# Seven products instead of plain matmuls for half of the second layer's last six channel tiles, and the mixer's coefficients computed earlier

## The chip, the cores and the metric

The kernel runs on one core of one Trainium2 chip. The metric is the device time of one execution in microseconds; the kernel before took 2144.43 us in the median of three runs (2143.85 to 2144.75). A profiled execution lies beside them and gives the views that are quoted here.

The core has five engines with queues of their own: TensorE (PE, with its weight loads as PEld), VectorE (DVE), ScalarE (ACT), GpSimd (POOL) and SyncE (SP). SP's queue issues nearly all DMAs, one after the other.

## What is computed

Two layers on 1024 tokens of 1024 channels, all in fp32. Each layer is a mixer (the first retention beside a gated delta rule, the second a gated linear recurrence) and a convolutional feed-forward block, both with residuals and RMS norms, and there is a norm at the end. Cut to what matters here:

```python
def rglru_mixer(hn, w_in, conv_w, conv_b, w_a, b_a, w_x, b_x, lam, w_out):
    ...
    r = jax.nn.sigmoid(jnp.einsum('btni,nij->btnj', xb, w_a) ... + b_a)
    i = jax.nn.sigmoid(jnp.einsum('btni,nij->btnj', xb, w_x) ... + b_x)
    log_a = -LRU_C * r * jax.nn.softplus(-lam)
    ...

def conv_ffn(hn, w_up, conv_w, conv_b, w_down):
    up = causal_dwconv(hn @ w_up, conv_w) + conv_b
    gate, val = jnp.split(up, 2, axis=-1)
    return (jax.nn.silu(gate) * val) @ w_down      # 2816 hidden channels to 1024

def reference(...):
    for layer in range(2):
        h = h + mixer(rms_norm(h, norm_mix[layer]))
        h = h + conv_ffn(rms_norm(h, norm_ffn[layer]), ...)
    return rms_norm(h, norm_final)
```

`softplus(-lam)`, `b_a` and `b_x` give the mixer's coefficients, a few columns of eight values.

## The kernel before, in words

Activations lie transposed, channels on the 128 partitions and tokens along the free axis: the residual is eight tiles `H[0]` to `H[7]` of 128x1024. Every fp32 matmul is made of three in the fast format: each operand is split into a high and a low part (ScalarE casts the high part, VectorE subtracts to get the low one), and `mm3` (L316 to L321) adds high x high, high x low and low x high into one PSUM bank.

**Seven products.** Where it can, the kernel takes a block of 2 x 2 matrices by seven products instead of eight (Strassen's scheme with few additions). The rows of the block are two groups of k tiles of the hidden channels, the columns are the even and the odd 256-token quarters (j = 0 and 1), and the outputs are a pair of output tiles. Seven operands, numbered o = 0 to 6, are made of the four blocks of activations and used for all pairs; `load_pair` (L283 on) makes the seven weight operands of a pair on VectorE. `pair_product` issues one product: three matmuls of 512 columns for each of its k tiles. `pair_added` adds each product into `H` on VectorE (L820).

**Feed-forward.** `ffn` first runs the up projection in 22 pairs p of output tiles (gate and value), 84 matmuls each; pair 0 in halves, since the norm's row comes late. After each pair, `hidden` computes the convolution and the gate and `store_parts` writes what the down projection will need to DRAM: ready splits to `p_dram` (high and low, L880), raw combinations to `s_dram` (L881), plain values to `y_dram`. The 22 hidden tiles make three sets c for the down projection: tiles 0 to 7, 8 to 15, and 16 to 21. `load_set(c, o)` brings operand o of a set back into SBUF, either as a ready split (L914) or raw, with a cast and a subtraction to follow (L922, L924, L925). The loads of set 0 begin while the last up pairs run, those of the next set while the fourth pair of outputs of the set before runs (`following` and `plain` say after which product).

In the first layer the third set is done by seven products too. In the second layer its six tiles are split whole by `store_parts` (L594, L595), written to `l_dram` (L870), loaded by `load_parts` (L931), and used by `final`: for each of the eight output tiles 6 k tiles, plain, in three column parts of 512, 256 and 256 tokens, with the residual added (L553) and squared (L407) as each tile is done. The norm of a part is `norm_beside` for the first (VectorE transposes and sums, a round through DRAM, the power on GpSimd: no TensorE), `norm_tok` and `norm_row` for the other two: strips of ones sum over partitions on TensorE (L480), VectorE turns them (L470, L471), GpSimd takes the power (L472), TensorE spreads the result as a row (L489). The tiles of a finished part are scaled (L1046) and stored between the tiles of the part that follows; of the first part every second one goes to ScalarE and GpSimd.

**Coefficients.** `lru_small` computes the second mixer's columns, some 29 operations of 128x8 on VectorE with one activation on ScalarE. It is called in the first layer's down projection, set 1, behind its first pair, into one of the four buffers of the pool `kept`.

**Order.** A scheduler places the instructions on each engine's queue by the order in which they were written and by when buffers come free, so a load can stand well ahead of the place that calls it; engines then work strictly through their queues. SP's queue holds all loads and stores of the places named here. The weights come six quarters ahead, in seven raw buffers.

Of the kernel before, what the change touches and what calls it, by code (L numbers as in the profile page):

```python
# [103 lines left out]
class Block:  # L104
    def __init__(self, ctx, tc, I, out, stop=None):
        self.ctx, self.tc, self.nc, self.I, self.out = ctx, tc, tc.nc, I, out
        nc = tc.nc
        pool = lambda n, b, **k: ctx.enter_context(tc.tile_pool(name=n, bufs=b, **k))
        self.perm = pool("perm", 1)
        self.wraw_p = pool("wraw", 7)  # L110
        self.kept = pool("kept", 4)
        self.parts = pool("parts", 1)
        self.wsp = pool("wsp", RING)
        self.tp = pool("tp", 3)
        self.sm = pool("sm", 2)
# [71 lines left out]
    def quarter_order(self):  # L187
# [10 lines left out]
        for layer in range(2):  # L198
# [11 lines left out]
            if layer == 0:  # L210
                o += [(("ffn_v0", t), 7) for t in range(4)]
# [611 lines left out]
    def ffn(self, layer, gain):  # L823
        nc, I = self.nc, self.I
        V, A = nc.vector, nc.scalar
        third = gain is not None
        sets = 3 if third else 2
        y_dram = self.tc.dram_tile([NPAIR, P, T], F32, name=f"yf_dram{layer}")
        s_dram = self.tc.dram_tile([sets, 5, 4, P, HALF], F32, name=f"sf_dram{layer}")

        p_dram = self.tc.dram_tile([sets, 4, 4, 2, P, HALF], F32, name=f"pf_dram{layer}")
        if not third:
            l_dram = self.tc.dram_tile([NPAIR - 16, 2, P, T], F32, name=f"lf_dram{layer}")
        depth = lambda c: 4 if c < 2 else 3

        def where(c, o):

            if c == 0 or not third:
# [24 lines left out]
        def store_parts(p, y, hi):  # L863
# [44 lines left out]
        def load_set(c, o):  # L908
# [17 lines left out]

        def load_parts(p):
            places = self.place2(p - 16)
            for n in range(2):
                for e in range(2):  # L930
                    nc.sync.dma_start(f32(places[n][e]), l_dram[p - 16, e][:, n * HALF:(n + 1) * HALF])  # L931
            return places
# [6 lines left out]
        def hidden(p, tg):  # L939
            tv = conv(NPAIR + p, self.halo[1])  # L940
            V.tensor_tensor(tg, tg, tv, ALU.mult)  # L941
            if (third or p < 16) and p % 8 < depth(p // 8):
# [25 lines left out]
        ys = {}  # L968
        following = {0: {1: (4, 5), **{o: ((o + 4) % 7,) for o in range(2, 7)}},
                     1: {2: (0,), 3: (1, 2), 4: (3,), 5: (4,), 6: (5, 6)}}  # L970
        plain = {0: {1: (0, 1), **{o: (o,) for o in range(2, 7)}}, 1: {}}
        for c in range(sets):
            done = self.down_steps(gain) if c == 2 else {}
            for t in range(4):
                sums, banks = self.pair_added(t), {}
                key = (f"ffn_w{layer}", c, t) if c < 2 else (f"ffn_v{layer}", t)
                for o in range(7):
                    sums(o, self.pair_product(banks, o, self.quarter(key, o), x=where(c, o)))
                    if t == 3 and c < 2:
                        for q in (following if third else plain)[c].get(o, ()):  # L980
                            load_set(c + 1, q)
                    if not third and (c, t) == (1, 3) and o in (1, 2):
                        for p in range(16, 20) if o == 1 else (20, 21):
                            ys[p] = load_parts(p)
# [4 lines left out]
                if third and (c, t) == (1, 0):  # L989
                    self.lru_small()  # L990

        if not third:
            self.final([ys[p] for p in range(16, NPAIR)], f"ffn_d{layer}")
# [44 lines left out]
    def final(self, ys, name):  # L1038

        nc = self.nc  # L1040
        V = nc.vector

# [9 lines left out]
        def part(t0, w, left):  # L1052

            sl = slice(t0, t0 + w)
            st = {"whole": t0 == 0}

            def each(m, h):
# [3 lines left out]
            self.part(ys, name, self.groups(1), sl, each, kept)  # L1061
            return st, sl


        kept = {}
# [6 lines left out]
        late[2].append(lambda: run(self.norm_tok(s1[0], 256)))  # L1072
        late[4].append(lambda: run(self.norm_row(s1[0], w=256)))
        pr = lambda st: st["row"][:, 0:256]
        for k in range(5, KT):
            late[k] += [lambda j=j: scale(*s1, j, pr(s1[0])) for j in range(3 * (k - 5), min(3 * (k - 4), KT))]
        s2 = part(768, 256, late)
# [12 lines left out]
    def lru_small(self):  # L1090

        V = self.nc.vector
        room = self.kept.tile([P, HALF], F32, tag="kept", name="lcols")
# [6 lines left out]
        V.tensor_scalar(nl, self.cols_of("lru_lam"), -1.0, None, ALU.mult)  # L1100
# [3 lines left out]
        V.tensor_scalar(ba, self.cols_of("lru_ba"), 0.5, None, ALU.mult)  # L1104
        V.tensor_scalar(bx, self.cols_of("lru_bx"), 0.5, None, ALU.mult)
# [737 lines left out]
    def _mix0_out(self, gain, gd):  # L1843
# [56 lines left out]
def _inputs(a):  # L1900
# [26 lines left out]
    for l in range(2):  # L1927
# [3 lines left out]
        if l == 0:  # L1931
            n = w.shape[0] // P - 16
            ins["ffn_v0"] = np.ascontiguousarray(w[2 * D:].reshape(n, P, KT, P).transpose(2, 1, 0, 3)).reshape(KT, P, n * P)
        else:
# [27 lines left out]
```

## Time and profile before

| what | us |
|---|---|
| median of three runs | 2144.43 |
| profiled execution, its own time | 2143.45 |
| span of its trace | 2141.7 |
| TensorE busy | 2126.3 |
| VectorE busy | 1722.0 |
| ScalarE busy | 1079.5 |
| GpSimd busy | 100.2 |

The span goes from the first to the last instruction. Matmuls are pipelined: one of 512 columns lasts 0.39 us in the records while the next begins after some 0.23, so TensorE's busy time is no measure of its pace; starts are. The granted clock of TensorE is full in all slices of the page. A wait row names the engine that waited and what released it.

### The profile page before, as it was taken

How to read it: one execution, taken by the hardware profiler on the slowest of the kernel's cores; microseconds unless marked ns; L12 is line 12 of the kernel's file. 1: busy time of each engine (PE TensorE's matmuls, PEld its weight loads, DVE VectorE, ACT ScalarE, POOL GpSimd, SP SyncE). 2: the span in 40 equal slices, each digit the busy share in tenths (PEclk: the TensorE clock that was granted, in tenths of full speed). 3: DMA queues.
4: the chain of work that ended last, by engine and by line, in shares of the span. 5: the costliest groups of instructions: out<-in, count | busy, mean ns of one | idle time of the engine just before them, and what ended most of it. 6: DMA issues, size and time to landing. Idle time of an engine off the chain costs nothing.

```text
span 2141.7 us, 29752 instructions
## 1 busy us (share of the span) xinstructions
PE 2126.3 (99%) x10648; PEld 1771.1 (83%) x10648; DVE 1722.0 (80%) x2630; ACT 1079.5 (50%) x1752; POOL 100.2 (5%) x115
## 2 busy tenths in 40 slices
PE   9999999999999999999999999999999999999998
PEld 7878888888888888887888888888888888888887
DVE  7995677766999989988868786768998989888645
ACT  6444422235665555555324576756655555554222
POOL 0102122300000000000000000000000000000002
PEclk9999999999999999999999999999999999999999
DMA  5354444543145445548745212152354444375542
GB/s 188 91 170 126 137 94 94 170 141 117 50 169 180 156 137 185 172 168 293 234 160 172 72 59 78 64 159 63 123 187 163 150 152 175 118 269 180 178 170 85
DMA packets 242021, 313.23 MB, mean 146 GB/s; under 512 B 62432, under 2 KB 129424, under 8 KB 241872
## 3 DMA queue, kind: packets, MB, share of 16 engines
q1 hardware_dynamic: 205632, 304.15, 43.0%
q10 hardware_dynamic: 35088, 6.36, 1.5%
q8 instruction: 84, 1.38, 0.3%
q0 software_dynamic: 1152, 0.81, 0.2%
q14 instruction: 65, 0.53, 0.1%
HBM read 215.79 MB, written 95.45 MB: 145 GB/s over the span
## 4 chain that ended last, share of the span: by engine, by line
PE 65%; issue 30%; DMA 2%; DVE 2%; POOL 1%; SPq 0%; ACT 0%; POOLq 0%; DVEq 0%
PE ps L319 19%; PE ps L321 19%; PE ps L320 19%; PE pc L319 1%; PE pc L321 1%; PE pc L320 1%; DMA raw<-in_mix_in_dram 0%; DMA s<-pf_dram 0%; PE ps L1644 0%; DMA l<-gc_dram 0%; PE pc L1552 0%; PE ps L1596 0%; PE pc L1664 0%; PE ps L1694 0%; PE pc L1578 0%
## 5 line engine op out<-in xcount | busy, mean ns | idle before, releaser
L319 PE MATMUL ps<-s,whi 128*128 128x512 f32 (+1 forms) x2692 | 1048.4, 390 | 1.0 <-ACT s L924 0.6
L320 PE MATMUL ps<-s,whi 128*128 128x512 f32 (+1 forms) x2692 | 1043.9, 388 | 1.9 <-DVE s L925 1.8
L321 PE MATMUL ps<-s,wlo 128*128 128x512 f32 (+1 forms) x2692 | 1042.6, 388 | 0.6 <-DVE wlo L273 0.6
L272 ACT CAST whi<-raw 128x512 fp32r<-128x512 f32 (+2 forms) x616 | 374.0, 613 | 607.7 <-PE ps L320 470.3
L319 PEld LDWEIGHTS ps<-s,whi 128*128 128x128 f32 x2692 | 505.6, 188 | 106.3 <-issue 1.8
L320 PEld LDWEIGHTS ps<-s,whi 128*128 128x128 f32 x2692 | 505.8, 188 | 105.6 <-DVE s L925 4.6
L321 PEld LDWEIGHTS ps<-s,wlo 128*128 128x128 f32 x2692 | 505.6, 188 | 104.4 <-DVE wlo L273 1.4
L273 DVE TENSOR_TENSOR wlo<-raw,whi 128x512 fp32r<-128x512 f32 (+2 forms) x616 | 414.1, 678 | 51.0 <-ACT whi L272 42.7
L852 DVE SCALAR_TENSOR_TENSOR t<-halo,cols,t 128x1024 f32<-128x1024 f32 x176 | 221.4, 1279 | 2.3 <-ACT t L850 1.0
L820 DVE TENSOR_TENSOR h<-ps,h 128x512 f32<-128x512 f32 x140 | 96.2, 688 | 74.4 <-PE ps L321 74.2
L810 DVE TENSOR_TENSOR halo<-ps,kept 128x512 f32<-128x512 f32 (+1 forms) x138 | 91.6, 664 | 71.1 <-PE ps L321 70.4
L850 ACT ACTIVATE t<-halo,cols 128x1024 f32<-128x1024 f32 x88 | 109.5, 1246 | 17.9 <-DVE halo L810 10.2
L805 ACT COPY kept<-ps 128x512 f32<-128x512 f32 (+1 forms) x138 | 76.9, 558 | 11.1 <-PE ps L321 9.6
L472 POOL TENSOR_TENSOR rtok<-rtok,npow 128x4 f32<-128x4 f32 (+1 forms) x10 | 9.9, 989 | 1095.3 <-DVE rtok L471 1095.3
L877 ACT CAST t<-t 128x512 fp32r<-128x512 f32 x68 | 41.2, 621 | 39.0 <-DVE t L941 37.0
L941 DVE TENSOR_TENSOR t<-t 128x1024 f32<-128x1024 f32 x44 | 53.5, 1217 | 0.0
L553 DVE TENSOR_TENSOR h<-ps,h 128x512 f32<-128x512 f32 (+1 forms) x48 | 28.5, 597 | 30.0 <-PE ps L321 29.9
L936 ACT ACTIVATE t<-t 128x1024 f32<-128x1024 f32 x44 | 46.8, 1063 | 10.3 <-DVE t L852 10.3
L882 DVE TENSOR_TENSOR t<-t 128x512 f32<-128x512 f32 x76 | 51.9, 683 | 0.0
L407 ACT ACTIVATE t<-h 128x512 f32<-128x512 f32 (+1 forms) x49 | 26.9, 563 | 45.4 <-DVE h L553 43.5
L878 DVE TENSOR_TENSOR lo<-t 128x512 fp32r<-128x512 f32 x68 | 46.4, 683 | 0.0
L379 DVE TENSOR_TENSOR halo<-ps,R 128x512 f32<-128x512 f32 x36 | 24.6, 685 | 26.8 <-PE ps L321 24.9
(342 smaller groups left out, 2189.4 us busy)
## 6 DMA issues: line engine op xcount, KB each, us to landing
raw<-in_ffn_up_dram SPq DMA_DIRECT2D x176, 256.0 KB, 2.7
s<-pf_dram SPq DMA_DIRECT2D x136, 256.0 KB, 4.8
sf_dram<-t SPq DMA_DIRECT2D x84, 256.0 KB, 2.5
pf_dram<-t SPq DMA_DIRECT2D x68, 256.0 KB, 2.6
pf_dram<-lo SPq DMA_DIRECT2D x68, 256.0 KB, 2.7
t<-sf_dram SPq DMA_DIRECT2D x67, 256.0 KB, 4.7
raw<-in_ffn_w_dram SPq DMA_DIRECT2D x64, 256.0 KB, 3.0
raw<-in_mix_in_dram SPq DMA_DIRECT2D x52, 256.0 KB, 3.2
```

Source lines behind the costliest of these rows:

```text
L272: self.nc.scalar.copy(hi[:, 0:w], raw[:, 0:w])
L273: eng.tensor_tensor(lo[:, 0:w], raw[:, 0:w], f32(hi[:, 0:w]), ALU.subtract)
L319: mm(ps, whi, xhi, start=start, stop=False)
L320: mm(ps, whi, xlo, start=False, stop=False)
L321: mm(ps, wlo, xhi, start=False, stop=stop)
L805: A.copy(kept[o], ps)
L810: V.tensor_tensor(dst(i, j), v(ps), v(kept[k]), ALU.add)
L820: V.tensor_tensor(h(*to[o]), ps.rearrange("p (h c) -> p h c", c=256), h(*to[o]), ALU.add)
L850: A.activation(t, buf[:, 2:2 + T], AF.Identity, scale=w(0), bias=self.col(f"ffn_cb{layer}", tile_i))
L852: V.scalar_tensor_tensor(t, buf[:, 2 + j:2 + j + T], w(j), t, ALU.mult, ALU.add)
L882: sub = lambda out, a, b: V.tensor_tensor(halves(out), a, b, ALU.subtract)
L941: V.tensor_tensor(tg, tg, tv, ALU.mult)
```

## The change

1. `lru_small` is called in the first layer's mixer, behind the gate of tile 4, and writes into a piece of permanent SBUF (`lru_room`) that was padding. Three of its operations are kept in the order of the program.
2. The second layer's third set is stored, like the first layer's, as parts; `l_dram` and `load_parts` are gone. Its first two pairs of outputs (tiles 0 to 3) are done by seven products with a weight array of its own.
3. `final` does output tiles 4 to 7 alone, plain, from the operands that are the plain blocks: 0 (j = 0) and an added one, 7 (j = 1, from `y_dram`), of the first three k tiles, 5 and 3 of the other three. Where operands lie in SBUF (`where`) and after which product they are loaded (`following`) is changed for this layer.
4. The squares of output tiles 0 to 3 are taken whole (128x1024) beside set 2's second pair and the first part of `final`. The first part's norm is now `norm_tok` and `norm_row` too, behind the tiles 4 and 5 of the second part, and all scalings are VectorE's, except the last two tiles of the last part.

```diff
@@ __init__
-        pad(self.perm, 96, "pad0")
+        self.lru_room = pad(self.perm, 96, "lru_room")
@@ quarter_order
-            if layer == 0:
-                o += [(("ffn_v0", t), 7) for t in range(4)]
+            o += [((f"ffn_v{layer}", t), 7) for t in range(2 if layer else 4)]
@@ ffn
-        if not third:
-            l_dram = self.tc.dram_tile([NPAIR - 16, 2, P, T], F32, name=f"lf_dram{layer}")
...
-            if o < 3:
-                i = (20, 14, 26)[o]
+            i = ((8, 0, 26, 6, 12, 0, 18, 20) if layer else (20, 14, 26, 0, 6, 12, 18))[o]
+            if o < 3 or o == 7:
                 return self.slots1(i, 6).rearrange("p (s n c) -> p n s c", n=2, c=256)
-            return self.s2[:, :, 6 * (o - 3):6 * (o - 2), :]
+            return self.s2[:, :, i:i + 6, :]
...
-            if p >= 16 and not third:
-                self.split_half(y, (hi, lo))
-                for e, t in enumerate((hi, lo)):
-                    nc.sync.dma_start(l_dram[p - 16, e], f32(t))
-                return
...
-                nc.sync.dma_start(r, s_dram[c, place[o], k])
+                if o < 7:
+                    nc.sync.dma_start(r, s_dram[c, place[o], k])
+                else:
+                    nc.sync.dma_start(halves(r), blocks(y_dram[16 + k])[:, :, 1])
...
-        following = {0: {1: (4, 5), **{o: ((o + 4) % 7,) for o in range(2, 7)}},
-                     1: {2: (0,), 3: (1, 2), 4: (3,), 5: (4,), 6: (5, 6)}}
-        plain = {0: {1: (0, 1), **{o: (o,) for o in range(2, 7)}}, 1: {}}
-        for c in range(sets):
-            done = self.down_steps(gain) if c == 2 else {}
-            for t in range(4):
+        following = {0: {1: (4, 5), **{o: ((o + 4) % 7,) for o in range(2, 7)}}, 2: {},
+                     1: {1: (1,), 3: (0, 2), 4: (5,), 5: (3,), 6: (4, 6)} if layer
+                     else {2: (0,), 3: (1, 2), 4: (3,), 5: (4,), 6: (5, 6)}}
+        for c in range(3):
+            done = {}
+            if c == 2:
+                done = self.final_steps() if layer else self.down_steps(gain)
+            for t in range(2 if layer and c == 2 else 4):
...
+                    if layer and (c, t, o) == (2, 0, 1):
+                        load_set(2, 7)
...
-                if third and (c, t) == (1, 0):
-                    self.lru_small()
+    def final_steps(self):
+        V, A = self.nc.vector, self.nc.scalar
+        self.acc, self.sq = self.t(), self.t()
+        def square(m):
+            def f():
+                if m == 0:
+                    A.activation(self.acc, self.H[m], AF.Square)
+                    return
+                A.activation(self.sq, self.H[m], AF.Square)
+                V.tensor_tensor(self.acc, self.acc, self.sq, ALU.add)
+            return f
+        self.squares = square
+        return {(1, 1): [square(0)], (1, 3): [square(1)]}
@@ final
+            for m in range(4, KT):
+                ps = self.pp(both=True)[:, 0:w]
+                for u in range(2):
+                    if (u, m) not in kept:
+                        kept[u, m] = self.load_kept(self.I[name + "ab"[u]][m], places[len(kept)])
+                    hi, lo = kept[u, m]
+                    for kt in range(4 - 2 * u):
+                        c = slice(kt * P, (kt + 1) * P)
+                        xh, xl = (operand(4 * u + kt, e, n, j) for e in range(2))
+                        self.mm3(ps, hi[:, c], lo[:, c], xh, xl, u == 0 and kt == 0, u == 1 and kt == 1)
...
-        s0 = part(0, 512, {})
-        R0 = self.R[:, 0:HALF]
-        self.norm_beside(s0[0], 0)
-        s1 = part(512, 256, {})
-        late = {k: [lambda k=k: scale(*s0, k, R0, nc.gpsimd if k % 2 else V)] for k in range(KT)}
+        s0 = part(0, 512, more, {4: [self.squares(2)], 5: [self.squares(3)]})
+        R0 = lambda: self.R[:, 0:HALF]
+        s1 = part(512, 256, self.sq[:, 0:HALF],
+                  {4: [lambda: run(self.norm_tok(s0[0]))], 5: [lambda: run(self.norm_row(s0[0], 0))],
+                   6: late(s0, (0, 1), R0), 7: late(s0, (2, 3), R0)})
+        s2 = part(768, 256, self.sq[:, HALF:],
+                  {4: late(s0, (4, 5), R0) + [lambda: run(self.norm_tok(s1[0], 256))],
+                   5: late(s0, (6, 7), R0) + [lambda: run(self.norm_row(s1[0], w=256))],
+                   6: late(s1, range(5), R1), 7: late(s1, range(5, 8), R1)})
@@ lru_small
-        room = self.kept.tile([P, HALF], F32, tag="kept", name="lcols")
+        room = self.lru_room
@@ _mix0_out
         for y in order:
             gate(y)
+            if y == 4:
+                self.lru_small()
```

Two places show how the instructions moved. The first is SP's queue in the second layer where up pair 20 ends (`pf_dram`, `sf_dram`, `yf_dram`, `lf_dram` are `p_dram`, `s_dram`, `y_dram`, `l_dram`; `s_96` and the other `s` are the two operand stores). Before:

```order
L870 DMA lf_dram_12997<-t 128x1024
L870 DMA lf_dram_12997<-lo 128x1024
L292 DMA raw<-in_ffn_w_dram 128x512 x3
L914 DMA s_12085<-pf_dram_12996 128x2x256 x10
L870 DMA lf_dram_12997<-t 128x1024
L870 DMA lf_dram_12997<-lo 128x1024
L914 DMA s_12085<-pf_dram_12996 128x2x256 x6
L922 DMA t<-sf_dram_12995 128x512 x3
```

And in the changed kernel (its line numbers differ by a few):

```order
L904 DMA s_12084<-pf_dram_12995 128x2x256
L884 DMA t<-yf_dram_12993 128x2x256
L885 DMA t<-sf_dram_12994 128x512
L904 DMA s_12084<-pf_dram_12995 128x2x256 x7
L870 DMA pf_dram_12995<-t 128x512
L870 DMA pf_dram_12995<-lo 128x512
L871 DMA sf_dram_12994<-t 128x512 x2
L870 DMA pf_dram_12995<-t 128x512
L870 DMA pf_dram_12995<-lo 128x512
L904 DMA s_12084<-pf_dram_12995 128x2x256
L871 DMA sf_dram_12994<-t 128x512
L904 DMA s_12084<-pf_dram_12995 128x2x256 x7
```

Ten operand loads stood ahead of this pair's two stores; now eight stand ahead of six of its seven stores, a ninth ahead of the last, and two loads of earlier parts are among them. The first layer's queue has the same rows at its own place, in both kernels.

The second place is VectorE in the second column part of `final`, between the additions of its tiles 5 and 7. Before:

```order
L553 TENSOR_TENSOR h_93<-ps,h_93 128x256
L411 TENSOR_TENSOR t<-t 128x256
L553 TENSOR_TENSOR h_94<-ps,h_94 128x256
L1046 SCALAR_TENSOR_TENSOR h_88<-h_88,cols,R 128x512
L411 TENSOR_TENSOR t<-t 128x256
L1046 SCALAR_TENSOR_TENSOR h_90<-h_90,cols,R 128x512
L1046 SCALAR_TENSOR_TENSOR h_92<-h_92,cols,R 128x512
L553 TENSOR_TENSOR h_95<-ps,h_95 128x256
```

After (`h_88` to `h_95` are `H[0]` to `H[7]`):

```order
L1080 TENSOR_TENSOR h_93<-ps,h_93 128x256
L410 TENSOR_TENSOR t<-t 128x256
L1047 SCALAR_TENSOR_TENSOR h_88<-h_88,cols,R 128x512
L1047 SCALAR_TENSOR_TENSOR h_89<-h_89,cols,R 128x512
L1047 SCALAR_TENSOR_TENSOR h_90<-h_90,cols,R 128x512
L1080 TENSOR_TENSOR h_94<-ps,h_94 128x256
L1047 SCALAR_TENSOR_TENSOR h_91<-h_91,cols,R 128x512
L410 TENSOR_TENSOR t<-t 128x256
L1047 SCALAR_TENSOR_TENSOR h_92<-h_92,cols,R 128x512
L1080 TENSOR_TENSOR h_95<-ps,h_95 128x256
```

Three scalings stood ahead of the last addition of this part, each of a second tile; now there are five, of consecutive tiles.

More of the change, by code (lines that the diff above doesn't have):

```diff
@@ L825, in ffn @@
         V, A = nc.vector, nc.scalar
-        third = gain is not None
-        sets = 3 if third else 2
         y_dram = self.tc.dram_tile([NPAIR, P, T], F32, name=f"yf_dram{layer}")
-        s_dram = self.tc.dram_tile([sets, 5, 4, P, HALF], F32, name=f"sf_dram{layer}")
-        p_dram = self.tc.dram_tile([sets, 4, 4, 2, P, HALF], F32, name=f"pf_dram{layer}")
-        if not third:
-            l_dram = self.tc.dram_tile([NPAIR - 16, 2, P, T], F32, name=f"lf_dram{layer}")
+        s_dram = self.tc.dram_tile([3, 5, 4, P, HALF], F32, name=f"sf_dram{layer}")
+        p_dram = self.tc.dram_tile([3, 4, 4, 2, P, HALF], F32, name=f"pf_dram{layer}")
         depth = lambda c: 4 if c < 2 else 3
         def where(c, o):
-            if c == 0 or not third:
+            if c == 0:
                 return self.operand(o)
@@ L941, in hidden @@
             V.tensor_tensor(tg, tg, tv, ALU.mult)
-            if (third or p < 16) and p % 8 < depth(p // 8):
+            if p % 8 < depth(p // 8):
                 nc.sync.dma_start(y_dram[p], tg)
@@ L978, in ffn @@
                     sums(o, self.pair_product(banks, o, self.quarter(key, o), x=where(c, o)))
-                    if t == 3 and c < 2:
-                        for q in (following if third else plain)[c].get(o, ()):
+                    if t == 3:
+                        for q in following[c].get(o, ()):
                             load_set(c + 1, q)
-                    if not third and (c, t) == (1, 3) and o in (1, 2):
-                        for p in range(16, 20) if o == 1 else (20, 21):
-                            ys[p] = load_parts(p)
+                    if layer and (c, t, o) == (2, 0, 1):
+                        load_set(2, 7)
                     for f in done.get((t, o), ()):
@@ L988, in ffn @@
                     hidden(NPAIR - 1, gate(NPAIR - 1))
-                if third and (c, t) == (1, 0):
-                    self.lru_small()
-        if not third:
-            self.final([ys[p] for p in range(16, NPAIR)], f"ffn_d{layer}")
+        if layer:
+            self.final(f"ffn_d{layer}")
+    def final_steps(self):
[11 more added lines that the diff above has]
+        return {(1, 1): [square(0)], (1, 3): [square(1)]}
     def down_steps(self, gain):
@@ L1036, in xplace, with final @@
         return ((0, 1, 2, 5, 3, 4, 6, 7)[k] * 4 + 2 * e) * HALF
-    def final(self, ys, name):
+    def final(self, name):
         nc = self.nc
         V = nc.vector
+        more = self.t()
         def scale(st, sl, k, pr, eng=V, queue=nc.sync):
@@ L1050, in scale, with operand, part @@
             queue.dma_start(self.out[k * P:(k + 1) * P, sl], h)
-        def part(t0, w, left):
-            sl = slice(t0, t0 + w)
-            st = {"whole": t0 == 0}
-            def each(m, h):
+        def operand(kt, e, n, j):
+            if kt < 3:
+                v = self.slots1(8, 24).rearrange("p (j s n c) -> p j s n c", j=2, s=12, n=2)[:, :, 3 * e + kt, n, :]
+            else:
+                v = self.s2[:, n, 0:12, :].rearrange("p (j s) c -> p j s c", j=2)[:, :, 3 * e + kt - 3, :]
+            return v if j is None else v[:, j, :]
+        kept, places = {}, [6, 14, 16, 18, 0, 2, 4, 26]
+        def part(t0, w, room, left):
+            sl = slice(t0, t0 + w)
+            n, j = t0 // HALF, None if w == HALF else t0 % HALF // 256
+            acc = self.acc[:, sl]
+            st = {"bufs": [acc] + [room[:, i * w:(i + 1) * w] for i in range(2)], "acc": [acc]}
+            for m in range(4, KT):
[8 more added lines that the diff above has]
+                        self.mm3(ps, hi[:, c], lo[:, c], xh, xl, u == 0 and kt == 0, u == 1 and kt == 1)
+                        self.slot()
+                h = self.H[m][:, sl]
+                V.tensor_tensor(h, ps, h, ALU.add)
                 self.square_step(st, m, h, w)
@@ L1060, in each @@
                     f()
-            self.part(ys, name, self.groups(1), sl, each, kept)
             return st, sl
-        kept = {}
         run = self.run
-        s0 = part(0, 512, {})
-        R0 = self.R[:, 0:HALF]
-        self.norm_beside(s0[0], 0)
-        s1 = part(512, 256, {})
-        late = {k: [lambda k=k: scale(*s0, k, R0, nc.gpsimd if k % 2 else V)] for k in range(KT)}
-        late[2].append(lambda: run(self.norm_tok(s1[0], 256)))
-        late[4].append(lambda: run(self.norm_row(s1[0], w=256)))
-        pr = lambda st: st["row"][:, 0:256]
-        for k in range(5, KT):
-            late[k] += [lambda j=j: scale(*s1, j, pr(s1[0])) for j in range(3 * (k - 5), min(3 * (k - 4), KT))]
-        s2 = part(768, 256, late)
+        late = lambda s, ks, row: [lambda k=k: scale(*s, k, row()) for k in ks]
+        s0 = part(0, 512, more, {4: [self.squares(2)], 5: [self.squares(3)]})
[3 more added lines that the diff above has]
+                   6: late(s0, (0, 1), R0), 7: late(s0, (2, 3), R0)})
+        pr = lambda st: st["row"][:, 0:256]
+        R1 = lambda: pr(s1[0])
+        s2 = part(768, 256, self.sq[:, HALF:],
+                  {4: late(s0, (4, 5), R0) + [lambda: run(self.norm_tok(s1[0], 256))],
+                   5: late(s0, (6, 7), R0) + [lambda: run(self.norm_row(s1[0], w=256))],
+                   6: late(s1, range(5), R1), 7: late(s1, range(5, 8), R1)})
         run(self.norm_tok(s2[0], 256))
```

21 lines of the change are left out of this document (7 added, 14 removed).

## The prediction

> **What bounds the kernel now.** I read the page first, its busy table.
>
> ```profile
> span 2141.7 us, 29752 instructions
> PE 2126.3 (99%) x10648; PEld 1771.1 (83%) x10648; DVE 1722.0 (80%) x2630; ACT 1079.5 (50%) x1752; POOL 100.2 (5%) x115
> ```
>
> TensorE is occupied for 2126.3 of 2141.7 us, so a matmul taken out counts in full, and so does every stretch in which the row of matmuls is held up. The overlap of matmuls hides short hold-ups from the busy share, so I next read the pace from starts, in a window of the last third of the second layer's down projection and in the timeline behind it.
>
> ```profile
> 2063.20:2095.86 32.66, 32.66 (x145) 27.03 (x144) 14.65 (x25) 11.02 (x21) 0.00 (x0) 1.00 0.25 87
> ```
>
> ```profile
> 2095.97 0.28 PE L320 MATMUL ps<-s,s 128*128 128x256 f32 x1
> 2103.89 0.28 PE L320 MATMUL ps<-s,s 128*128 128x256 f32 x1
> ```
>
> In a window's row stand its length, then each engine's busy time with the instructions that touch it (TensorE first, VectorE third, ScalarE fourth), the granted clock, the DMA share and GB/s. The window holds 144 starts of 512 columns (145 touch it) in 32.66 us, 0.2268 each. Between the two timeline rows lie 22 groups of three at 256 columns: 7.92 us, 0.120 each, a little more than half (0.28 is the length of one, not the step).
>
> **The change part by part. Products.** The grouping of that last third, 2063.2 to 2131.9, gives the counts.
>
> ```profile
> L319 PE MATMUL ps<-s,s 128*128 128x256 f32 x96 | 27.3, 285 | 0.0
> L319 PE MATMUL ps<-s,s 128*128 128x512 f32 x48 | 18.7, 389 | 0.0
> ```
>
> Each line stands for three equal ones (L319 to L321): before, 144 matmuls at 512 and 288 at 256 columns, 32.6 + 34.6 = 67.2 us. After: two pairs of output tiles by seven products of nine matmuls, 126 at 512, and for output tiles 4 to 7 the plain way, 72 at 512 and 144 at 256: 198 x 0.2267 + 144 x 0.120 = 44.9 + 17.3 = 62.2 us. Removed: 5.0 us.
>
> **The norm of the first half moves onto TensorE.** Before, it goes through VectorE, GpSimd and DMA; now eight strip sums and four row matmuls stand among the 256-wide matmuls. The first layer has the same pieces:
>
> ```profile
> 1203.95 0.39 PE L319 MATMUL ps<-s,whi 128*128 128x512 f32 x1
> 1204.27 0.64 PE L480 MATMUL pc<-t,ones 128*32 128x128 f32 x16
> 1205.18 0.40 PE L321 MATMUL ps<-s,wlo 128*128 128x512 f32 x1
> 1206.91 0.64 PE L480 MATMUL pc<-t,ones 128*32 128x128 f32 x16
> 1208.05 0.40 PE L321 MATMUL ps<-s,wlo 128*128 128x512 f32 x1
> 1208.29 1.05 PE L489 MATMUL pc<-ident,rtok 128*128 128x128 f32 x8
> 1208.36 1.01 POOL L472 TENSOR_TENSOR rtok<-rtok,npow 128x4 f32<-128x4 f32 x1 [0.70 <-DVE rtok L471]
> 1209.41 0.39 PE L320 MATMUL ps<-s,whi 128*128 128x512 f32 x1
> ```
>
> Sixteen records are eight matmuls, since one of fp32 stands as two. From 1203.95 to 1205.18 run two ordinary matmuls and the strips: 1.23 - 0.45 = 0.78 us. From 1208.05 to 1209.41 two ordinary ones and the row: 1.36 - 0.45 = 0.91. Added: 1.7 us. The row matmul also waits for the power on GpSimd: from strips to its end 1206.91 to 1209.37, 2.46 us, and the new VectorE order puts one 256-wide addition (0.42) into it. TensorE reaches the row 0.78 + 18 x 0.120 = 2.94 us after the strips began, so the cover is just enough; I put 0.1 for it, bounds 0 and 1.0 (the power once more).
>
> **The tail.** Sixteen scalings, of which the last quarter formerly held most over 16.6 us, now share two quarters of about 9 us with the additions and squares.
>
> ```profile
> 2113.70 0.75 DVE L1046 SCALAR_TENSOR_TENSOR h<-h,cols,R 128x512 f32<-128x512 f32 x1 [2.10 <-DMA R<-nrow_dram]
> 2119.54 1.43 DVE L1046 SCALAR_TENSOR_TENSOR h<-h,cols,R 128x512 f32<-128x512 f32 x1
> 2113.89 6.53 POOL L1049 TENSOR_TENSOR h<-h,R 128x512 f32<-128x512 f32 x4 [6.11 <-DMA R<-nrow_dram]
> 2126.30 1.65 DVE L1046 SCALAR_TENSOR_TENSOR h<-h,cols,pc 128x256 f32<-128x256 f32 x4
> ```
>
> At 0.75 for a scaling of 512 and 0.41 for one of 256, VectorE has 8 x 0.75 + 8 x 0.41 + 14 x 0.4 = 15 us of work in some 19 us; walking its new order through, it comes to the last addition about when TensorE has finished, 0 to 1 us late. So what follows the last wide matmul stays as it is. The slow 1.43 stands where GpSimd scales too, and that use of GpSimd is gone. The Trainium skill (SBUF — State Buffer, "Who interferes with whom") says why: a VectorE operation with two SBUF inputs and a GpSimd one that reads SBUF lock each other out; the trace agrees (0.75 alone, 1.43 beside). With the contended price throughout (0.41 stretched alike to 0.78) the work would be 23.3 us, 4.3 too many: the bound of this term.
>
> **The operands of the down projection.** This is the term that decides. Six tiles that used to be kept as plain halves are now stored as parts like all others, in the second layer as in the first. I compared the two layers at the seam from up to down projection, in windows shifted by 925 us, the distance between the same matmul in both:
>
> ```profile
> 566.36 0.28 PE L321 MATMUL ps<-s,wlo 128*128 128x256 f32 x1
> 1491.25 0.28 PE L321 MATMUL ps<-s,wlo 128*128 128x256 f32 x1
> ...
> 986.00:996.00 10.00, 9.77 (x43) 7.42 (x42) 7.43 (x25) 2.79 (x5) 0.00 (x0) 1.00 1.06 368
> 996.00:1011.00 15.00, 12.53 (x50) 8.71 (x49) 12.61 (x20) 10.42 (x16) 0.00 (x0) 1.00 0.88 323
> 1911.00:1921.00 10.00, 10.00 (x46) 8.29 (x45) 6.73 (x11) 5.25 (x10) 0.00 (x0) 1.00 1.07 389
> 1921.00:1936.00 15.00, 14.72 (x64) 11.36 (x63) 14.48 (x22) 9.70 (x15) 0.00 (x0) 1.00 0.71 237
> ```
>
> The first layer starts 93 matmuls in its 25 us, the second 110: seventeen fewer at 0.2267, 3.8 us. Why:
>
> ```profile
> 979.92 0.32 SPq L881 DMA_DIRECT2D sf_dram<-t  x1
> 980.29 4.71 SPq L914 DMA_DIRECT2D s<-pf_dram  x7
> 997.40 1.87 ACT L924 CAST s<-t 128x512 fp32r<-128x512 f32 x3 [5.52 <-DMA t<-sf_dram]
> 998.07 0.49 PE L319 MATMUL ps<-s,whi 128*128 128x512 f32 x1 [0.56 <-ACT s L924]
> 1918.22 1.86 ACT L924 CAST s<-t 128x512 fp32r<-128x512 f32 x3 [4.64 <-DMA t<-sf_dram]
> s<-pf_dram SPq DMA_DIRECT2D x16, 256.0 KB, 4.6
> s<-pf_dram SPq DMA_DIRECT2D x22, 256.0 KB, 4.9
> ```
>
> In the first layer the stores of the last pairs stand ahead of the loads in SP's one queue until 979.92; by the end of the up projection it has issued 16 of the operand loads (40 us to 986), the second layer 22 (40 us to 1911). Six loads of 256 KB at 368 GB/s are 4.3 us, and the cast that the fifth product needs comes at 997.40, after TensorE wanted it; shifted by 925, the second layer's is 4.2 us earlier. The change's order of SP in the second layer is now row for row that of the first up to the last third. So I carry the first layer's price over: +3.8, bounds 0 and 4.6 (first layer's whole loss: 93 starts against 113 at full pace). The Trainium skill (DMA: Bandwidth & Descriptors, "Specifications") gives a core about 358 GB/s of HBM; the windows show 323 to 389, so the trace agrees that the queue is at its limit, and by that figure the six loads would be 4.4 us.
>
> Two more seams follow, where the first layer loses a little and the second nothing:
>
> ```profile
> 1061.00:1081.00 20.00, 20.00 (x89) 16.19 (x88) 9.05 (x15) 5.05 (x9) 0.00 (x0) 1.00 1.08 389
> 1142.00:1157.00 15.00, 14.80 (x66) 11.97 (x65) 12.22 (x23) 6.17 (x12) 0.00 (x0) 1.00 0.63 212
> 1986.00:2006.00 20.00, 20.00 (x90) 16.57 (x89) 12.82 (x20) 6.20 (x11) 0.00 (x0) 1.00 0.80 288
> ```
>
> One matmul short of 90, and two of 68: +0.2 and +0.4 (bounds 0 and 1.5: the last third's loads differ from the first layer's, and three tile loads stand between them in SP's queue).
>
> **The coefficients** move from that seam of the first layer into its mixer.
>
> ```profile
> L1221 DVE TENSOR_TENSOR lcols<-lcols x7: 161/168/169, 985.4 to 993.3; 128x8 f32<-128x8 f32 x7
> 982.84 1.28 ACT L1214 ACT_TABLE_LOAD   x1
> 981.61 0.16 DVE L1100 TENSOR_SCALAR lcols<-cols 128x8 f32<-128x8 f32 x1
> 450.00:460.00 10.00, 10.00 (x45) 8.27 (x45) 6.39 (x8) 3.24 (x5) 0.00 (x0) 1.00 0.38 103
> ```
>
> 29 operations at 0.17 us and a gap behind most are some 5.5 us of VectorE, and two table loads 2.6 us of ScalarE. In the mixer VectorE idles 3.6 us in each 10 and TensorE waits for nothing there, so they cost nothing; without that cover it would be 5.5 us. At the old place they begin at 981.61, after the store of 979.92 that let the loads go, so the late loads do not come from them: I take a gain of 0, bound 3.7 (the first layer falling to the second's loss).
>
> **Sum.** -5.0 + 1.7 + 0.1 + 3.8 + 0.6 = +1.2, and -0.2 for a short wait in the old last quarter: +1.0. The profiled execution took 2143.45 us, 1.75 more than its span; the median of the three is 2144.43, 1.0 above it. So 2144.4 as profiled, 2145.4 as median.
>
> **Rivals.** (1) The second layer's operands come in time all the same, since its loads have the buffers free earlier: -2.8 in all, 2141.6. For it speaks that its slack was 4 us; against it that the queue's order is the first layer's. (2) The first layer's loss was due to the coefficients on VectorE after all (they lie between its subtractions from 981 to 994), so it shrinks to the second's and the second keeps its own: -2.8 - 3.7 = -6.5, 2137.9. For it speaks the place; against it the order of 979.92 and 981.61. (3) Slower: the tail. VectorE becomes the bound of the two last quarters, the last addition waits behind the scalings; it decides once the work exceeds 19 us, that is from about 1.1 us for a scaling of 512 and 0.6 for one of 256. At the contended 1.43 and 0.78 it is 4.3 on top of my sum: 2149.7. Only GpSimd's share made them slow, so I doubt it. (4) The change does not do what it says: the removed matmuls were not on the path. With TensorE at 99% I leave almost nothing: the rest would be +6, 2150.
>
> **Chances.** Forecast 0.62 (own range 2143.4 to 2147.5); rival 1 0.18; rival 2 0.10; rival 3 0.08; rival 4 0.02. Tell-apart is about 0.2%, 4.3 us. Faster: rival 2 and a corner of rival 1, 0.13; slower: 3 and 4, 0.10; the rest within, 0.77. The range goes from rival 1 to the upper end of the seams, 2141.0 to 2148.3, which leaves out rivals 2 to 4.
>
> **What would show it.** Right: in the second layer's first 25 us of the down projection the starts fall from 110 to about 93, with casts waiting for the sf load; the first layer's windows keep 93; 62 us of wide matmuls at the end. Wrong: the second layer keeps over 105 (rival 1), the first rises over 105 (rival 2), or the last addition starts over 1 us after TensorE is done (rival 3).

## The result: 1.0% slower, and almost every matmul of one buffer takes longer

The changed kernel takes 2165.88 us in the median of four runs (2165.53 to 2167.22), the kernel before 2144.47 beside it: ratio 1.0101, 95% interval 1.0088 to 1.0114. The forecast was 2145.4, within 2141.0 to 2148.3. It is 18 us away from the nearer end, and none of its rivals tells of such a loss.

The page after, span and busy table:

```profile
span 2163.7 us, 29782 instructions
PE 2145.8 (99%) x10582; PEld 1763.0 (81%) x10582; DVE 1744.0 (81%) x2672; ACT 1083.5 (50%) x1763; POOL 93.5 (4%) x107
```

The first sign stands here. There are 66 records of TensorE fewer than before (10582 against 10648), and yet it is busy 19.5 us longer. A long wait shows as idle time and not as busy time, so the loss is not in long waits at a seam: the matmuls themselves take longer. The granted clock is full in every slice, so the throttle did not do it. The next view is the windows of a stretch that the change does not touch, the first layer's up projection from 600 to 900 us, for before and for after:

```profile
600.00:900.00 300.00, 300.00 (x1325) 248.37 (x1325) 273.63 (x369) 172.30 (x254) 0.00 (x0) 1.00 0.49 169
```

```profile
600.00:900.00 300.00, 300.00 (x1307) 244.69 (x1306) 270.19 (x364) 168.83 (x248) 0.00 (x0) 1.00 0.48 166
```

TensorE never idles in either, but starts 1324 matmuls in one and 1306 in the other: 0.2266 us each before, 0.2297 after (one or two of the number that a row shows began ahead of the window, so these means are good to about 0.2 ns). A view of the operand tiles in two short stretches of the changed kernel shows which matmuls are slow (names without their digits, so that `s` is `s1` as well as `s2`):

```profile
L320 PE MATMUL ps<-s,wlo x9: 394/394/394, 702.8 to 708.4; 128*128 128x512 f32 x9
...
L320 PE MATMUL ps<-s,wlo x11: 389/389/389, 711.9 to 718.7; 128*128 128x512 f32 x11
```

In the first row the line comes nine times from 702.8 to 708.4: eight steps of three matmuls, 5.6 us by 24, 0.2333 each. In the second it is ten steps of three from 711.9 to 718.7, 0.2267 each. The pace changes in blocks of 36 and 48 matmuls, and that is the program's pattern: of the 84 matmuls of an up pair, 48 read their activations (the operand whose 512 columns stream through) from the buffer `s1` and 36 from `s2`. So the places that the allocator gave are the next thing to compare, in bytes of a partition:

```
           before    after
s1          37376    37376    a multiple of 512 in both
nblk       179648    (gone)   128 bytes
nbt        179776    (gone)   128 bytes
ntok       179904    (gone)    64 bytes
s2         179968   179648    256 over a multiple of 512; now 448 over one
```

The kernel before works out the row of the first part's norm in three small tiles of the pool `sm` (`small("nblk", 32), small("nbt", 32), small("ntok", 16)`, in `norm_beside`). The change calls `norm_beside` no more, the three tiles fall away, and everything allocated behind them moves down by 320 bytes. That is `s2` and, in the mixers, the buffers that share its room. 2724 matmuls of 512 columns read `s2`, in both layers from some 400 us on.

### The profile page after: what moved, and what is told of

Read it like the earlier page. It is cut to its first block, busy times and chain, and to the rows that moved or that the text cites. A ratio compares the mean times of both kernels' runs of the same rounds, so it can differ in the third digit from the quotient of the medians.

```text
span 2163.7 us, 29782 instructions
## 1 busy us (share of the span) xinstructions
PE 2145.8 (99%) x10582; PEld 1763.0 (81%) x10582; DVE 1744.0 (81%) x2672; ACT 1083.5 (50%) x1763; POOL 93.5 (4%) x107
## 4 chain that ended last, share of the span: by engine, by line
PE 94%; DMA 2%; DVE 2%; issue 1%; SPq 0%; POOL 0%; ACT 0%; POOLq 0%; DVEq 0%; ACTq 0%
PE ps L318 28%; PE ps L319 28%; PE ps L320 28%; DMA t<-sf_dram 1%; DMA s<-pf_dram 1%; PE pc L318 1%; PE pc L319 1%; PE pc L320 1%; PE ps L1666 0%; PE ps L1668 0%; PE ps L1667 0%; PE pc L488 0%; SPq L904 0%; PE pc L479 0%; PE ps L1618 0%
## 5 line engine op out<-in xcount | busy, mean ns | idle before, releaser
L318 PE MATMUL ps<-s,whi 128*128 128x512 f32 (+1 forms) x2734 | 1070.1, 392 | 1.5 <-ACT s L917 1.1
L319 PE MATMUL ps<-s,whi 128*128 128x512 f32 (+1 forms) x2734 | 1066.3, 390 | 3.4 <-DVE s L918 2.9
L320 PE MATMUL ps<-s,wlo 128*128 128x512 f32 (+1 forms) x2734 | 1063.4, 389 | 1.3 <-DVE wlo L272 1.3
L319 PEld LDWEIGHTS ps<-s,whi 128*128 128x128 f32 x2734 | 513.3, 188 | 117.5 <-DVE s L918 7.5
L318 PEld LDWEIGHTS ps<-s,whi 128*128 128x128 f32 x2734 | 513.1, 188 | 117.6 <-ACT s L917 3.1
L320 PEld LDWEIGHTS ps<-s,wlo 128*128 128x128 f32 x2734 | 513.0, 188 | 113.3 <-DVE wlo L272 2.1
L272 DVE TENSOR_TENSOR wlo<-raw,whi 128x512 fp32r<-128x512 f32 (+2 forms) x630 | 422.5, 677 | 50.9 <-ACT whi L271 43.4
L819 DVE TENSOR_TENSOR h<-ps,h 128x512 f32<-128x512 f32 x154 | 105.9, 689 | 81.0 <-PE ps L320 80.3
L872 DVE TENSOR_TENSOR t<-t 128x512 f32<-128x512 f32 x88 | 60.2, 685 | 1.2 <-DMA sf_dram<-t 1.2
L868 DVE TENSOR_TENSOR lo<-t 128x512 fp32r<-128x512 f32 x80 | 54.8, 685 | 0.0
L917 ACT CAST s<-t 128x512 fp32r<-128x512 f32 x57 | 35.3, 620 | 31.0 <-DMA t<-sf_dram 21.3
L293 DVE TENSOR_TENSOR raw<-raw 128x512 f32<-128x512 f32 (+1 forms) x66 | 44.7, 678 | 2.8 <-issue 1.3
```

Source lines behind the costliest of these rows:

```text
L272: eng.tensor_tensor(lo[:, 0:w], raw[:, 0:w], f32(hi[:, 0:w]), ALU.subtract)
L318: mm(ps, whi, xhi, start=start, stop=False)
L319: mm(ps, whi, xlo, start=False, stop=False)
L320: mm(ps, wlo, xhi, start=False, stop=stop)
L819: V.tensor_tensor(h(*to[o]), ps.rearrange("p (h c) -> p h c", c=256), h(*to[o]), ALU.add)
L868: V.tensor_tensor(halves(lo[:, at]), src, f32(halves(hi[:, at])), ALU.subtract)
```

## The experiments

The theory after this look, **address**: the 320 bytes cost about 18 us, and the rest is what the forecast's terms make. The rival, **work**: transfers or other engines beside the matmuls slow them, and the address is a coincidence. One kernel moves `s2` back in the changed kernel, the other moves it away in the kernel before.

### The change with `s2` back in its place

```diff
@@ __init__ of the changed kernel, behind the pool sm
+        pool("gap", 1).tile([P, 80], F32, name="gap")
```

> The changed kernel with one unused tile of 320 bytes per partition ahead of the operand buffer s2, nothing else: the changed kernel no longer uses the three small tiles nblk, nbt and ntok (128 + 128 + 64 bytes) of the row worked out beside the products, so that s2 moved down from byte 179968 to 179648 of its partition; the tile moves it back. Theory 'address': the trace of the change has 226 to 227 ns from one 512-column matmul to the next where the operand lies in s1 and 233 to 234 ns where it lies in s2, and before has 226 to 227 for both. 2724 matmuls of 512 columns read s2, 2724 x 6.67 ns = 18.2 us: this run has no step of 233 ns, and takes 2165.9 - 18.2 = 2147.7 us (2145 to 2149). Rival 'work': the longer steps come from the work beside them (ports, transfers, order), the address has no part in it: 2165.9 again (2164 to 2167).

Measured: 2147.55 us, 18.3 below the change; ratio to before 1.0014 (1.0005 to 1.0023). The stretch has its old pace back:

```profile
600.00:900.00 300.00, 300.00 (x1325) 248.32 (x1324) 273.62 (x369) 172.18 (x254) 0.00 (x0) 1.00 0.49 169
```

An unused tile gives back 18.3 of 21.4 us.

### The kernel before with `s2` moved

```diff
@@ __init__ of the kernel before, behind the pool sm (48 floats; 32, 16 and 8 in three more kernels)
+        pool("gap", 1).tile([P, 48], F32, name="gap")
```

> The kernel before with one unused tile of 192 bytes ahead of s2, nothing else: s2 at byte 180160, 448 over a multiple of 512, as in the changed kernel. Theory 'address': its 2760 matmuls of 512 columns that read s2 take 6.67 ns more each, 18.4 us: 2162.9 us (2161 to 2165). Rival 'work': 2144.5 (2143 to 2146).

Measured: 2165.02 us, at the upper end of what was expected; ratio 1.0093 (1.0080 to 1.0107). Nothing but an unused tile of 192 bytes makes the kernel before as slow as the change. Rival **work** falls with this pair.

### Which places are slow

> The kernel before with an unused tile of 128 bytes ahead of s2: s2 at byte 180096, 384 over a multiple of 512, a multiple of 128. s2 lay 256 over a multiple of 512 before (fast) and 448 over one after (slow). If multiples of 128 are enough, the steps stay at 226 to 227 ns and the time at 2144 us; if it has to be a multiple of 256, the steps that read s2 are longer, and the time is near 2163 us when they are as long as in the change.

> s2 at 180032, 320 over a multiple of 512 (64 over one of 256). If all that is no multiple of 256 costs the same: mean step of 229.7 to 229.8 ns between 600 and 900 us as at 384 and 448, 2163 us. If the price grows with what the rows reach into the next 256 bytes, it is another mean than at 384 and 448.

> s2 at 180000, 288 over a multiple of 512 (32 over one of 256, no multiple of 64). If any place off a multiple of 256 costs one more access per row: 229.7 to 229.8 ns again. If 64 bytes are a unit of their own, it is slower than the others, above 2165 us.

> The changed kernel with an unused tile of 64 bytes ahead of s2: s2 at 179712, a multiple of 512. If a multiple of 256 is what the rows need (256 over a multiple of 512 is fast, 384 and 448 are slow): steps of 226 to 227 ns, 2147 us.

These four kernels gave one time each, without an interval, and so did the one with moved weights below. The windows of the same stretch, one kernel each, `s2` at 192, 128, 64 and 32 bytes over a multiple of 256, and last the changed kernel with 64 unused bytes (16 floats in the same place), where `s2` starts on a multiple of 512:

```profile
600.00:900.00 300.00, 300.00 (x1308) 244.65 (x1307) 270.24 (x363) 168.82 (x248) 0.00 (x0) 1.00 0.48 166
```

```profile
600.00:900.00 300.00, 300.00 (x1308) 245.17 (x1308) 270.25 (x364) 168.89 (x248) 0.00 (x0) 1.00 0.48 166
```

```profile
600.00:900.00 300.00, 300.00 (x1315) 246.51 (x1314) 271.78 (x366) 170.10 (x250) 0.00 (x0) 1.00 0.48 166
```

```profile
600.00:900.00 300.00, 300.00 (x1306) 244.73 (x1305) 269.78 (x364) 168.50 (x248) 0.00 (x0) 1.00 0.48 166
```

```profile
600.00:900.00 300.00, 300.00 (x1325) 248.31 (x1324) 273.69 (x370) 172.40 (x255) 0.00 (x0) 1.00 0.49 170
```

| `s2` over a multiple of 256 | mean of all matmuls there, ns | time, us |
|---|---|---|
| 0 (before: 256 over 512) | 226.6 | 2144.5 |
| 0 (a multiple of 512, changed kernel) | 226.6 | 2147.5 |
| 192 (before, moved) | 229.5 | 2165.0 |
| 192 (the change) | 229.7 | 2165.9 |
| 128 | 229.5 | 2163.1 |
| 64 | 228.3 | 2157.3 |
| 32 | 229.9 | 2166.5 |

(The mean is 300 us by the starts of the row; three in seven of these matmuls read `s2`, so one of those costs 7/3 of the difference.) Both multiples of 256 are fast, the four other places are slow, 128 bytes as much as 192. The price is not the same everywhere: 64 bytes over costs a little over half of what the others do, though 192 is an odd multiple of 64 as well. My reading of "one more access per row" doesn't explain that, and why 64 is milder stays open.

### The weights moved by 64 bytes

```diff
@@ __init__ of the changed kernel
+        pool("gap", 1).tile([P, 16], F32, name="gap")
         self.wsp = pool("wsp", RING)
+        pool("gap2", 1).tile([P, 48], F32, name="gap2")
...
+        pool("gap3", 1).tile([P, 16], F32, name="gap3")      # behind sm: s2 at 179968
```

> The changed kernel with unused tiles of 64 bytes ahead of the weight parts whi and wlo and 256 behind them: s2 at 179968 as before, but all weight parts 64 bytes over a multiple of 256. Theory 'moving operand' (the rows that stream through TensorE are read slower, the weights are loaded beside them in 188 ns of 227): steps of 226 to 227 ns and about 2147 us. If weights count as the moving operand does: all 512-column steps at 233 ns, 8200 x 6.67 ns = +55 us.

Measured: 2195.76 us, 48 above the realigned kernel, where the second theory had 55. The theory that only the streamed operand counts was wrong. The windows row of the same stretch, one line's matmuls in a short stretch, and this kernel's weight loads from the groups of instructions:

```profile
600.00:900.00 300.00, 300.00 (x1289) 241.75 (x1288) 268.03 (x360) 169.73 (x251) 0.00 (x0) 1.00 0.47 164
```

```profile
L323 PE MATMUL ps<-s,wlo x9: 393/393/398, 702.8 to 708.4; 128*128 128x512 f32 x9
```

```profile
L322 PEld LDWEIGHTS ps<-s,whi 128*128 128x128 f32 x2734 | 513.9, 188 | 125.4 <-DVE s L921 6.8 <-DMA s<-pf_dram 0.4 <-issue 0.2
```

All matmuls are at 300 by 1288, 0.2329 us; counted by the starts of one line, as above, eight steps of three take 5.6 us, 0.2333 each, which is the slow pace of `s2`. A weight load still lasts 188 ns in the records, as in the kernel before, and is shorter than a step; the records of the loads do not show the price, the steps do. The Trainium skill (SBUF — State Buffer, "Who interferes with whom") gives TensorE two read ports that don't depend on each other, one for the streamed operand and one for the weights. If that is read to mean that a load which takes no longer and is hidden under the step costs nothing, this run shows 48 us, and the measurement decides. No run moves the streamed operand and the weights by the same amount, so whether each place counts by itself or the difference between the two is not shown.

### Layer 2's operands: is the seam's loss due to transfers?

With `s2` in its place the forecast's own terms can be seen. The seam from up to down projection in the realigned kernel, in the prediction's windows, shifted by what it is late at the landmarks that the prediction used (0.1 us in the first layer, 1.4 in the second):

```profile
986.10:996.10 10.00, 9.60 (x40) 6.85 (x39) 4.85 (x8) 2.57 (x5) 0.00 (x0) 1.00 1.05 368
996.10:1011.10 15.00, 12.54 (x50) 8.64 (x49) 11.87 (x19) 10.29 (x15) 0.00 (x0) 1.00 0.88 323
1912.40:1922.40 10.00, 9.37 (x38) 6.61 (x37) 4.83 (x8) 2.58 (x5) 0.00 (x0) 1.00 1.06 377
1922.40:1937.40 15.00, 12.54 (x50) 8.66 (x50) 11.55 (x18) 9.91 (x15) 0.00 (x0) 1.00 0.88 319
```

The second layer's 110 starts have become 88, near the first layer's 90. SyncE's rows show what stands ahead of the loads: pair 20's seven stores of parts, which the transfers have to move in the same microseconds. Pair 20 is the last but one of the up projection; its own reads and stores are some 2.3 MB.

```profile
1894.91 4.45 SPq L905 DMA_DIRECT2D s<-pf_dram  x7
1900.39 0.33 SPq L871 DMA_DIRECT2D pf_dram<-t  x1
1901.54 0.33 SPq L871 DMA_DIRECT2D pf_dram<-lo  x1
1901.92 0.93 SPq L872 DMA_DIRECT2D sf_dram<-t  x2
1902.94 0.56 SPq L871 DMA_DIRECT2D pf_dram<-t  x1
1903.59 0.62 SPq L871 DMA_DIRECT2D pf_dram<-lo  x1
1904.30 0.89 SPq L905 DMA_DIRECT2D s<-pf_dram  x1
1907.10 0.32 SPq L872 DMA_DIRECT2D sf_dram<-t  x1
1907.47 4.53 SPq L905 DMA_DIRECT2D s<-pf_dram  x7
1912.05 1.54 SPq L914 DMA_DIRECT2D t<-sf_dram  x3
```

The transfers are not all of it: SP's queue also stands still until the parts are made. Behind the load that ends at 1905.19 it waits for VectorE until 1907.10, and from 1892 to 1913 its waits for pair 20's parts add up to 4.1 us.

The third set needs these parts only some 150 us later. So three kernels store pair 20's hidden tile as it is (one store of 512 KB) and make its parts later:

```diff
@@ hidden (LATE holds layer and pair)
-            if p % 8 < depth(p // 8):
+            if p % 8 < depth(p // 8) or (layer, p) in LATE:
                 nc.sync.dma_start(y_dram[p], tg)
-            store_parts(p, tg, tv)
+            if (layer, p) not in LATE:
+                store_parts(p, tg, tv)
@@ the down projection's loop, behind set 1's second pair
+                    if (layer, p) in LATE and (c, t) == at:
+                        y = self.t()
+                        nc.sync.dma_start(y, y_dram[p])
+                        store_parts(p, y, self.t())
```

> The realigned kernel (change plus the unused tile); in layer 2 the last but one pair (20) stores only its hidden tile before the down projection (0.5 MB), and its parts are made and stored in the down projection's second set, from the tile read back. That takes 2 reads and 7 or 8 stores of 256 KB each, 2.3 MB less the 0.5 MB, out of the time just ahead of the first operands' loads. Theory 'transfers' (the prediction's term of +3.8 us, PE waits of 5.6 us at this seam in the realigned run against 0.87 before): 1.8 MB at the 390 GB/s of those windows is 4.6 us, the waits fall to about 1 us, and the time from 2147.6 to 2143.2 (2142 to 2144.5). Rival 'VectorE': per product four subtractions of 0.68 and one addition of 0.69 are 3.4 us against 12 matmuls of 0.227 = 2.72, and set the seam whenever the loads land: the waits stay above 3 us, 2145.5 or more.

> The same in both layers. Layer 1's seam is the model that the prediction took for layer 2's: theory 'transfers': its waits of 5.3 us fall to about 1 too, 2139 us (2137.5 to 2141). Rival 'VectorE': 2144 or more.

> Pairs 19 and 20 put off in both layers. Theory 'transfers': the waits that are left at the two seams go as well, if the parts made later (in the second set's first two output pairs) hide there: 2138 (2136.5 to 2140). If VectorE or the queue cannot hide them in the second set, it is above late20_both.

Measured: 2141.61 us for the second layer alone (ratio 0.9985, 0.9977 to 0.9994), 2137.22 for both layers (0.9965, 0.9952 to 0.9979), 2138.20 with pair 19 as well (0.9970, 0.9958 to 0.9981). SyncE's rows of the first, the same place (it runs 0.8 us earlier here):

```profile
1893.48 4.49 SPq L909 DMA_DIRECT2D s<-pf_dram  x7
1898.95 0.33 SPq L934 DMA_DIRECT2D yf_dram<-t  x1
1899.33 4.85 SPq L909 DMA_DIRECT2D s<-pf_dram  x7
1904.24 1.55 SPq L918 DMA_DIRECT2D t<-sf_dram  x3
```

The queue's waits for pair 20 are down to 0.9 us. The first reads of `sf_dram` that follow are issued 7.8 us earlier, 7.0 beyond what the whole kernel is ahead. The seam of the second layer in this kernel, and of the first layer in the one that does both:

```profile
1911.60:1936.60 25.00, 25.00 (x112) 20.71 (x111) 21.55 (x34) 15.31 (x26) 0.00 (x0) 1.00 0.82 288
```

```profile
985.50:1010.50 25.00, 25.00 (x112) 20.72 (x111) 21.86 (x35) 15.77 (x26) 0.00 (x0) 1.00 0.83 285
```

111 starts in 25 us is full pace. So the seam's loss comes from pair 20's stores ahead of the loads, as the theory **transfers** has it. That it is their bytes alone is not shown: the edit takes away 1.8 MB and also 3.2 us for which the one queue stood still for parts not yet made (from 1892 to 1912 the transfers run at 269 GB/s in the realigned kernel and at 319 in this one), and no run parts the two. The theory's bytes were 4.6 us and were to leave 1 us of waits; none are left, and the first two times lie below their expected ranges. **VectorE**, by the expectation 3.4 us per product on the operands against TensorE's 2.72, would have kept more than 3 us of waits and is refuted as it was put. Putting off pair 19 too finds nothing left to gain.

### How much of that does the change have a part in?

> The kernel before with pair 20 of layer 1 put off in the same way, nothing of the change. If putting off is worth the same 4 to 4.6 us there (waits of 4.6 us at its seam gone): 2140.2 us (2139 to 2141.5), and what the change itself gives beyond it, in the kernel with both put off (2137.2), is 3 us: the 5.0 of the products less the 1.7 of the norm. If it gives less here, more of the 7.6 us between the change in line (2147.6 on its chip) and the one with both put off comes from the change.

```diff
@@ hidden, kernel before, first layer only
-            store_parts(p, tg, tv)
+            if not (third and p == 20):
+                store_parts(p, tg, tv)
```

(with the same store of the hidden tile, and the same later place for the parts.) Measured: 2139.37 us, ratio 0.9974 (0.9964 to 0.9984), 5.4 us below before. That is more than the 4 to 4.6 us that were expected of it, though inside the expected range. Its interval overlaps that of the change with both put off (0.9965): of the 3 us that the change should give beyond, the medians show 2, and the two were not run on the same chip. The change with 320 unused bytes and pair 20 late in both layers has the lowest median of all kernels here, but that the change itself has a part in it is not shown.

### The coefficients alone

```diff
@@ the kernel before: the call moves, nothing else
-                if third and (c, t) == (1, 0):
-                    self.lru_small()
...
             gate(y)
+            if y == 4:
+                self.lru_small()
```

> The kernel before with the coefficient operations alone moved from layer 1's down projection into the mixer; s2 stays where it was. Prediction's forecast: covered in the mixer and not what ends the seam's waits, 2144.5 (2143.5 to 2145.5). Its second rival: the VectorE work is what made layer 1's first operands late, and its removal gives back up to 3.7 us: 2140.8 (2140 to 2142.5). If the mixer does not cover them: up to +5.5.

Measured: 2144.80 us, ratio 1.0001 (0.9992 to 1.0010). The first layer's seam in this kernel:

```profile
986.00:996.00 10.00, 9.31 (x37) 6.43 (x37) 4.55 (x7) 2.48 (x4) 0.00 (x0) 1.00 1.05 362
996.00:1011.00 15.00, 12.55 (x50) 8.64 (x49) 12.17 (x19) 10.35 (x15) 0.00 (x0) 1.00 0.88 325
```

VectorE is freed of its small operations there (from 25 and 20 instructions to 7 and 19), and TensorE starts no more than before: 87 against 93. The prediction's second rival falls. The six starts fewer are 1.2 us more of waits by the steps, and the realigned kernel's 90 point the same way; whether the move costs something is too small for the times here to show.

## Why the prediction was wrong, point by point

**The step that failed** is one that the sum does not have. "The norm of the first half moves onto TensorE" counted what `norm_beside` issued and what replaces it, and not that three tiles cease to be allocated. All terms took 0.2267 us for a matmul of 512 columns from the trace of before, as though a matmul kept its pace when its operands move. The two kernels with nothing but an unused tile show -18.3 us for the change and +20.9 for before. By the windows: (229.7 - 226.6) x 7/3 = 7.2 ns for each of 2724 matmuls, 19.7 us, near enough; the two short stretches (0.2333 and 0.2267) give 6.7 ns and 18.2 us. Laid side by side, the traces of the change and of the realigned kernel, with the same matmuls in the same order, drift apart from some 400 us on, by 17.3 us at the last matmul. The row that could have warned was not in the profile: the source has tiles called `pad0`, `pad1` and `pad2` that nothing reads, and I asked nothing of why they are there.

**Without that term** the sum stands at the realigned kernel's 2147.55 against the forecast 2145.4, inside its range. It is 3.5 us above the kernel before of its own chip (2144.09), where the sum has 1.0. The sum's terms, from the last matmul of the second layer's first norm to the last strip sums, of before and of the realigned kernel:

```profile
1491.25:2132.98 641.73, 640.33 (x3058) 537.88 (x3057) 524.39 (x736) 311.94 (x476) 9.35 (x10) 1.00 0.47 161
```

```profile
1492.66:2137.57 644.91, 640.08 (x2993) 531.00 (x2991) 543.93 (x778) 318.89 (x489) 2.36 (x3) 1.00 0.51 174
```

The realigned trace is 4.7 us longer in all. Of that 3.2 lie in this stretch and 0.1 behind it; the other 1.4 lie ahead of it, 0.7 of them at the first layer's seam, and the sum has no term for them.

- **Products and norm, -5.0 + 1.7 + 0.1 - 0.2: right.** Adding up the steps of TensorE over 245 ns, less 227 ns each, the realigned kernel waits 6.7 us more in this stretch (4.7 at the seam, 1.9 in the two later seams). What is left of the 3.2 is -3.5, against -3.4 by the sum.
- **The tail, 0: right.** From the last strip sums to the end are 8.7 us before and 8.8 in the realigned kernel. The scalings that the change puts on VectorE take 748 ns in the median, not 1.43 us, with GpSimd out of the way, and TensorE's last waits (0.7 and 1.5 us) are those of before (0.7 and 1.4). The third rival falls. (The 0.75 us that the prediction calls alone overlaps the start of GpSimd's first scaling, 2113.70 against 2113.89; the row below is the cleaner reading.) The row of scalings:

```profile
L1048 DVE SCALAR_TENSOR_TENSOR h<-h,cols,R x8: 745/748/752, 2123.2 to 2128.9; 128x512 f32<-128x512 f32 x8
```

- **The operands at the seam, +3.8: mechanism right, size a little low.** From 110 to 88 starts is 5.0 us (4.7 by the steps), over the upper bound of 4.6, since the copy went a little further than the first layer's 93. The runs with pair 20 put off show that the stores ahead of the loads are the cause, by their transfers, by the queue's waits for them, or by both, and the first rival falls. The 358 GB/s that the prediction quotes for a core are no limit here: its own rows reach 389, and it is well that its sum goes by the rows.
- **The two later seams, +0.6: too low.** The steps show 1.9 us in the second layer, over the bound of 1.5. One of the waits there is for ScalarE's cast of a weight (0.48 us), which the first layer does not have at that place.
- **The coefficients, 0: right by the time** (1.0001), though the first layer's windows fall from 93 starts to 87 with that move alone and to 90 in the realigned kernel, where the prediction had them keep 93.
- **The fourth rival** (the removed matmuls were not on the path) falls with the first point.

Seams and products together leave the change about 3 us slower than before, as the interval 1.0005 to 1.0023 has it. So even the change in line does not pay by itself; what it saves on TensorE it gives back in waits for its operands. With pair 20's parts out of the way it may be worth some 2 us, which the intervals do not part from nothing.

## What to carry to other kernels

A change that drops or adds a tile moves all that is allocated behind it, and a moved matmul operand can cost more than the change is about: compare the places of the matmuls' operands in both programs before costing anything. Here streamed operands and weights on multiples of 256 bytes were fast, and every other place that was run was slow. When a part of the work grows that nobody touched, look at the pace from start to start there first. And what must be stored only for a later stage should not stand in front of the loads that the next stage waits for.

## What I had not expected of the hardware

- A matmul of 512 columns in the fast fp32 format whose streamed operand (two runs of 256 values) starts on a multiple of 256 bytes follows the one ahead after 0.2267 us; 192 bytes off it is 0.2333, with the same work beside it, full clock and TensorE busy throughout.
- The same holds for the weights, though their load (188 ns) is shorter than the step and as long as before: 64 bytes off made the steps of the same stretch 0.2333 us from start to start (0.2329 by the windows row), 48 us over the kernel.
- The price differs with the place (228.3 to 229.9 ns over the mixed stretch), and 64 bytes off is the mildest. What part of the chip pays it no run here shows.
